# Attention output weights and two gate rows: prepared before the attention stage, or inside the branch stage

## The chip, the cores and the metric

The kernel runs on one core of a Trainium2 chip. A core has five engines that run their own instruction queues side by side: TensorE (PE, matrix products), VectorE (DVE, elementwise work and scans), ScalarE (ACT, copies, casts and activations), GpSimd (POOL) and SyncE (SP, which here only issues transfers). ACT can issue transfers too; an instruction of its queue that has to wait holds up everything behind it. The transfers of all queues run on 16 DMA engines. The metric is the device time of one execution in microseconds (us), as the median of the runs; lower is better.

## What is computed

One step of a one-layer encoder over 1024 prompt frames and 32 sampled frames, 1056 columns in all (`T`), model width 1024:

```
h = rmsnorm(x, g_mix);  q, k, v, cb, cc, cx, ga, gc = split(h @ w_in)
y_attn = stick_breaking(q, k, v) @ w_attn_out        # 512 -> 1024
y_conv = (cb * causal_conv(cc * cx)) @ w_conv_out    # 512 -> 1024
merged = sigmoid(ga) * y_attn + sigmoid(gc) * y_conv
x = x + merged @ w_o
x = x + square(relu(rmsnorm(x, g_ffn) @ w_up)) @ w_down
x = x + sigmoid(rmsnorm(x, g_ple) @ w_ple_gate) * (p @ w_ple)
```

Activations lie transposed, channels on the 128 partitions. A "row" below is a block of 128 channels by 1056 columns (528 KB). The gate `ga` has rows 0 to 7, and so has `gc`; row n of `gd` in DRAM holds row n of `ga`, row n + 8 that of `gc`.

## The kernel before

**Number format.** Every float32 product is made of three matmuls: an operand is split into a high half (a cast by ACT) and a low half (a subtraction by DVE, operand minus high half). So a weight tile costs one ACT and one DVE instruction before PE can use it, and the third matmul of a group is the first that needs the low half.

**Stages.** (1) The input projection runs over pairs of output rows, `SETS` (products named `ps_...i17` for the last pair, gate rows 6 and 7). `seven` does a pair with seven half-size products, and small tasks in the list `side` run one piece after each product. (2) Attention, about 403 to 617 us of the span: 64 steps over 4 head pairs, 2 heads each and 8 query blocks (n is the step's number). Step n makes the scores `z` (PE, line 861), ACT turns them into `r` by a sigmoid (L865), POOL masks them, DVE runs a scan (L879), PE transposes (`pa`, L915), ACT and DVE split the result into `at` (L918, L919), and PE gathers (`av`, L936). There is one buffer for `z` in PSUM, so the next `z` waits until ACT has read the last one. Between the steps PE works off a plan of other products (`fill`), at the start the gate products `ps_g` of rows 0 to 3. (3) The branch stage, about 617 to 687 us, goes through `SEQ_B`: four rows of the convolution output (`c`) and the eight of the attention output (`a`), each of 36 matmuls of 352 columns. For a row, `branch_fetch` loads the weight and the gate row, `branch_high` and `branch_low` split the weight (L984 on ACT, L992 on DVE), `branch_scale` and `branch_sigmoid` finish the gate (L1002 on DVE, L1007 on ACT), `branch_post` multiplies the product by the gate (L1018), `merge_add` adds both branches (L1021), and `merge_high`, `merge_low` and `merge_sums` make the operands of the next stage (L1027, L1031, L1051 to L1059). Six PSUM buffers lie between PE and `branch_post`. (4) The output projection (`ps_woA`, `ps_woS`), from 687 us, whose weights are split at L1561 and L1565. The MLP and the last gate follow, to the end of the span.

**What sets the order.** The order on PE, ACT, DVE and POOL is the order in which the code issues (the blocks under `manual_schedule`). Transfers on SP's queue are placed by a scheduler. All transfers go round eight semaphores; a transfer issued by ACT waits in ACT's queue until the earlier transfer on its semaphore has landed.

**The early tasks.** While the last pair of the input projection runs, `ahead_gate(4)` and `ahead_gate(5)` load gate rows 4 and 5 from `gd`, scale them by the norm factor (DVE), take the sigmoid (ACT) and store them to `gs_`. `ahead_attn(4..7)` load attention output weights 4 to 7, split them and store both halves to `aod`. Both stores are issued by ACT (L649, L638). In the branch stage these rows then need no scale, no sigmoid and no split: the halves come from `aod` as one load (`raw_oa`, L973), and `READY` lists the gate rows that are finished before that stage. The last two gate rows, 6 and 7, stay in SBUF (`last_m`, tiles `m1_i17` and `m2_i17`); they are scaled at attention steps 3 and 4, and at steps 5 and 6 ACT takes the sigmoid and stores them (L1362, L1363).

Of the kernel before, what the change touches and what calls it, by code (L numbers as in the profile page):

```python
# [9 lines left out]
F32 = mybir.dt.float32  # L10
F32R = mybir.dt.float32r
AF = mybir.ActivationFunctionType
# [3 lines left out]
P = 128  # L16
D = 1024
KD = D // P
SEQ = 1024
DEC = 32  # L20
T = SEQ + DEC
# [18 lines left out]
AT2 = (0, 4, 5, 8, 10, 14)  # L40
NEARLY = 4
AT_IN = (4, 8, 10, 12, 14, 18)
READY = (4, 5, 6, 7, 8, 9, 10, 11, 14, 15)
CFILL = 4
ORDER = "LSAFBFG"
START = 2.5
SQ_AT = 96
AHEAD = 6
MM = {mybir.EngineType.Activation, mybir.EngineType.PE, mybir.EngineType.DVE, mybir.EngineType.Pool}


# [1 line left out]
def tile_step(  # L53
# [8 lines left out]
    nc = tc.nc  # L62
# [3 lines left out]
    wraw = ctx.enter_context(tc.tile_pool(name="wraw", bufs=RB))  # L66
    wsp = ctx.enter_context(tc.tile_pool(name="wsp", bufs=2))
    dpool = ctx.enter_context(tc.tile_pool(name="dpool", bufs=1, space=bass.MemoryType.DRAM))

    def blk(name, dt=F32, shape=None):  # L70
        return bpool.tile(shape or [P, T], dt, tag="B", name=name)
# [28 lines left out]
    def raw_w(w, n, kb, name):  # L100
        raw = wraw.tile([P, kb, P], F32, tag="raw", name=f"raw_{name}")
        nc.sync.dma_start(raw, w[n])
        return raw
# [36 lines left out]
    add, sub = ALU.add, ALU.subtract  # L140
    dve, pool = nc.vector.tensor_tensor, nc.gpsimd.tensor_tensor
    raws, ws, side = {}, {}, []
# [174 lines left out]
    def after(n, *gens):  # L317
        for _ in range(n):
            yield
        for g in gens:  # L320
            yield from g
# [15 lines left out]
    SETS = [("g", 12), ("g", 4)] + [(nm, 0) for nm in ("cc", "cx", "cb", "q", "k", "v")] + [("g", 8)]  # L337
# [140 lines left out]
    def md(k, s_):  # L478
        return md_[k, s_ // NP_][s_ % NP_]

    gs_ = dpool.tile([2, P, T], F32, name="gs_")
    aod = dpool.tile([KD, P, 2, 4 * P], F32, name="aod")
    xd = dpool.tile([KD, P, T], F32, name="xd")
    xe = dpool.tile([KD, P, T], F32, name="xe")
    td = [dpool.tile([KD // 2, P, T // 2], F32, name=f"td{k}") for k in range(4)]
# [40 lines left out]
    def scaled(m, by=None):  # L526
        if by is None:
            dve(m, m, rs, op=ALU.mult)
        else:
            nc.vector.scalar_tensor_tensor(m, m, by, rs, op0=ALU.mult, op1=ALU.mult)  # L530
# [89 lines left out]
    def gate_done(n, m):  # L620
        scaled(m)
        yield
        yield
        nc.scalar.activation(m, m, AF.Sigmoid)
        nc.sync.dma_start(gd[n], m)
        yield

    def ahead_attn(n):
        t = blk(f"ao{n}", F32R, [P, 2, 4, P])
        raw = t[:, 1].bitcast(F32)  # L630
        nc.sync.dma_start(raw, w_attn_out[n])
        for _ in range(5):
            yield
        nc.scalar.copy(t[:, 0], raw)
        dve(t[:, 1], raw, t[:, 0].bitcast(F32), op=sub)
        yield
        yield
        nc.scalar.dma_start(aod[n], t.bitcast(F32).rearrange("p e k n -> p e (k n)"))  # L638
        yield

    def ahead_gate(n):
        m = blk(f"ga{n}")
        nc.sync.dma_start(m, gd[n])
        for _ in range(5):
            yield
        scaled(m)
        yield
        nc.scalar.activation(m, m, AF.Sigmoid)
        nc.scalar.dma_start(gs_[n - 4], m)  # L649
        yield  # L650

    def follow(nm, n, ms, wait=0):
# [313 lines left out]

    def branch_fetch(b):
        nm, n = b
        if nm == "c" or n < 4:
            w = raw_w(w_conv_out if nm == "c" else w_attn_out, n, 4, f"o{nm}{n}")  # L970
        else:
            w = wraw.tile([P, 2, 4, P], F32R, tag="raw", name=f"raw_o{nm}{n}")
            nc.sync.dma_start(w.bitcast(F32).rearrange("p e k n -> p e (k n)"), aod[n])  # L973
        sg = blk(f"s{nm}{n}")
        nc.sync.dma_start(sg, gd[n + 8] if nm == "c" else gs_[n - 4] if n in (4, 5) else gd[n])
        fetched[b] = w, sg

    def branch_high(b):
        nm, n = b
        if nm == "a" and n > 3:  # L980
            made[b] = tuple(fetched[b][0][:, i] for i in range(2))
            return
        hi = wsp.tile([P, 4, P], F32R, tag="whi", name=f"whi_o{nm}{n}")
        nc.scalar.copy(hi, fetched[b][0])  # L984
        made[b] = hi

    def branch_low(b):
        nm, n = b
        if nm == "a" and n > 3:
            return  # L990
        lo = wsp.tile([P, 4, P], F32R, tag="wlo", name=f"wlo_o{nm}{n}")
        dve(lo, fetched[b][0], made[b].bitcast(F32), op=sub)  # L992
        made[b] = made[b], lo
# [231 lines left out]
    with tc.manual_schedule(engines=MM):  # L1225
        nc.scalar.preload_act_table_set("sqrt_and_others")
        run(first_gates())
        for s_ in range(2, len(SETS)):
            nm, n = SETS[s_]
            if s_ == 2:  # L1230
                side.append(after(1, stats_x()))
            elif s_ == 4:
                nc.scalar.preload_act_table_set("sigmoid_and_others")
            elif s_ == len(SETS) - 1:
                side.extend(after(AHEAD + i // 2, ahead_gate(n)) for i, n in enumerate((4, 5)))
                side.extend(after(AHEAD + 1 + i // 2, ahead_attn(n)) for i, n in enumerate(range(4, 8)))
            if s_ + 1 < len(SETS):
                side.append(prepare(f"i{s_ + 1}", AT_IN))
            else:
                side.extend([after(4, second_parts(0)), after(6, second_parts(1)), after(4, call(hooks_to, -20)), after(10, call(hooks_to, 0))])  # L1240
            if s_ + 2 < len(SETS):
                side.append(after(5, call(fetch_in, s_ + 2)))
            m = blk(f"m1_i{s_}"), blk(f"m2_i{s_}")
            run(seven(f"i{s_}", *m, copy_of))
            if s_ + 1 < len(SETS):
                follow(nm, n, m, 6 * (s_ == 2))
            else:
                last_m = n, m
        keys_values(0, 0)
        pools[:] = [gps]  # L1250
        run(ahead(START))
        while side:
            run(range(1))
# [99 lines left out]
    with tc.manual_schedule(engines=MM):  # L1353
        queries(0, 0, 0)
        queries(0, 0, 1)
        for n in range(LAST + 3):
            done_f, parts = 0, None
            if n in (3, 4):
                scaled(last_m[1][n - 3])
            elif n in (5, 6):  # L1360
                m = last_m[1][n - 5]
                nc.scalar.activation(m, m, AF.Sigmoid)  # L1362
                nc.scalar.dma_start(gd[last_m[0] + n - 5], m)  # L1363
            if n == 1:
                sample_loads()
            elif n == 3:
                sample_keys()
            if n < LAST:
                i = steps[n][2]
                if i % 2 == 0 and n + 4 < LAST:  # L1370
                    p_, j_, i_ = steps[n + 4]
                    queries(p_, j_, i_ // 2)
                if i == 2 and n + 8 < LAST:
                    keys_values(*steps[n + 8][:2])
            for op in ORDER:
                if op == "S" and n < LAST:
                    scores(*steps[n])
                    if n == LAST - 1:
                        zf = zps.tile([P, 2, 512], F32, tag="z", name="zf")
                        spare_ps.extend(zf[:, h, :] for h in range(2))  # L1380
                elif op == "L":
                    if 1 <= n <= LAST:
                        weigh(*steps[n - 1])
                    for f in pending + split_low:
                        f()
                    pending.clear()
                    split_low.clear()
                elif op == "F" and n < LAST + 2:
                    done_f += 1
                    fill(share[n] + (share[n + 1] - share[n]) * done_f / nf)  # L1390
                    if done_f == 1 and n in SAMPLE_AT:
                        next(sample, None)
                elif op == "G" and n >= 3 and steps[n - 3][2] % 2 == 1:
                    p, j, i_ = steps[n - 3]
                    gather(p, j, i_ // 2)
                elif op in "AB" and 2 <= n <= LAST + 1:
                    if op == "A":
                        parts = flip(*steps[n - 2])
                    next(parts, None)
# [1008 lines left out]
```

## Time and profile before

| | |
|---|---|
| device time, median of 3 runs | 1540.46 us (1539.76 to 1541.39) |
| the profiled execution | 1543.13 us, span from first to last instruction 1541.4 us |
| PE busy | 1511.6 us, 98% of the span |
| DVE, ACT, POOL busy | 1131.5, 763.0, 280.9 us |
| mean granted TensorE clock | 0.995 |
| transfers | 286.83 MB, mean 186 GB/s |

All times below are us from the start of the span. A row of the timeline gives start, duration, engine, line, operation, the tile written and the tiles read (buffer numbers left out), shape and count; in brackets stands how long the engine was idle before the row and who released it. "SPq" and "ACTq" rows are transfers being issued. A row of the windows gives for each engine the busy time and the instructions in that stretch, then the granted TensorE clock, the share of the 16 DMA engines in use and GB/s.

### The profile page before, as it was taken

What the parts mean: (1) busy time and instruction counts of PE and PEld (TensorE: products, weight loads), DVE (VectorE), ACT (ScalarE), POOL (GpSimd) and SP (SyncE); (2) the same over time, 40 slices, a digit from 0 to 9 for tenths busy, and PEclk for the clock granted to TensorE, in tenths of its full rate; (3) what the DMA queues carried; (4) which work ended last, traced back from release to release, by engine and by line L of the source; (5) the groups of instructions that cost most, each with busy time, mean ns of one, the idle gap of its engine ahead of it and who ended that gap; (6) DMA issues with size and microseconds to landing.
All of it is one profiled execution on the core that took longest, in us unless ns stands there. A gap on an engine that the chain in (4) does not pass through costs nothing.

```text
span 1541.4 us, 29904 instructions
## 1 busy us (share of the span) xinstructions
PE 1511.6 (98%) x11888; PEld 1498.2 (97%) x11888; DVE 1131.5 (73%) x1597; ACT 763.0 (50%) x1415; POOL 280.9 (18%) x318
## 2 busy tenths in 40 slices
PE   8999999999899999999999999999999999999997
PEld 8999999999789999999999999999999999999997
DVE  7568666657578988799876677675576986799756
ACT  6544444434456666333375556645543334434654
POOL 2123322231012212000002113222020220000253
PEclk9999999999999999999999999999999999999999
DMA  6513445413946752446755455544886897673443
GB/s 223 202 51 114 190 153 193 166 45 132 311 133 191 253 164 92 168 162 224 267 182 173 159 171 209 193 154 154 300 282 200 277 332 240 205 274 121 140 127 118
DMA packets 121036, 286.83 MB, mean 186 GB/s; under 512 B 13856, under 2 KB 34592, under 8 KB 120896
## 3 DMA queue, kind: packets, MB, share of 16 engines
q1 hardware_dynamic: 119456, 280.34, 54.3%
q10 hardware_dynamic: 1440, 4.58, 0.7%
q8 instruction: 93, 1.52, 0.4%
q14 instruction: 47, 0.39, 0.1%
HBM read 200.98 MB, written 83.89 MB: 185 GB/s over the span
## 4 chain that ended last, share of the span: by engine, by line
PE 59%; DVE 2%; ACT 1%; issue 1%; DMA 0%; SPq 0%; DVEq 0%; ACTq 0%
PE ps_dn L1993 7%; PE ps_dn L1991 7%; PE ps_dn L1992 7%; PE ps_woA L1709 4%; PE ps_A11u L244 2%; PE ps_A11u L242 2%; PE ps_A11u L243 2%; PE ps_pg L120 2%; PE ps_pg L121 2%; PE ps_pg L122 2%; PE ps_S1u L243 2%; PE ps_S1u L244 2%; PE ps_S1u L242 2%; PE ps_woS L1709 2%; PE ps_oa L120 1%; PE ps_oa L122 1%
## 5 line engine op out<-in xcount | busy, mean ns | idle before, releaser
L1993 PE MATMUL ps_dn<-fh,wlo_dn 128*128 128x264 f32 x896 | 255.4, 285 | 0.0
L1992 PE MATMUL ps_dn<-fl,whi_dn 128*128 128x264 f32 x896 | 254.9, 284 | 0.0
L1991 PE MATMUL ps_dn<-fh,whi_dn 128*128 128x264 f32 x896 | 254.8, 284 | 0.0
L1991 PEld LDWEIGHTS ps_dn<-fh,whi_dn 128*128 128x128 f32 x896 | 168.9, 188 | 0.0
L1993 PEld LDWEIGHTS ps_dn<-fh,wlo_dn 128*128 128x128 f32 x896 | 168.8, 188 | 0.0
L1992 PEld LDWEIGHTS ps_dn<-fl,whi_dn 128*128 128x128 f32 x896 | 168.6, 188 | 0.0
L209 POOL TENSOR_TENSOR s_u<-raw_u,raw_u 128x512 f32<-128x512 f32 x22 | 32.1, 1461 | 359.6 <-DVE slS_u L170 284.6
L879 DVE TENSOR_TENSOR_SCAN r<-r 128x128 f32<-128x128 f32 (+3 forms) x64 | 86.5, 1351 | 2.8 <-POOL r L872 2.8
L209 POOL TENSOR_TENSOR s_i<-raw_i,raw_i 128x512 f32<-128x512 f32 x32 | 44.2, 1380 | 239.4 <-DVE slS_i L170 210.3
L1878 ACT CAST whi_dn<-raw_dn 128x1024 fp32r<-128x1024 f32 x40 | 42.0, 1051 | 84.9 <-PE ps_dn L1992 80.9
L1884 DVE TENSOR_TENSOR wlo_dn<-raw_dn,whi_dn 128x1024 fp32r<-128x1024 f32 x40 | 60.9, 1523 | 29.0 <-ACT whi_dn L1878 28.9
L919 DVE TENSOR_TENSOR at<-pa,at 128x512 fp32r<-128x512 f32 (+2 forms) x96 | 52.0, 550 | 31.5 <-ACT at L918 26.9
L242 PE MATMUL ps_A11i<-T,shS_i 128*128 128x264 f32 x256 | 73.1, 286 | 0.0
L244 PE MATMUL ps_A11i<-T,slS_i 128*128 128x264 f32 x256 | 73.0, 285 | 0.0
L243 PE MATMUL ps_A11i<-T,shS_i 128*128 128x264 f32 x256 | 72.8, 284 | 0.0
L170 DVE TENSOR_TENSOR slS_i<-s_i,shS_i 128x512 fp32r<-128x512 f32 x48 | 34.8, 731 | 50.0 <-ACT shS_i L168 49.9
L1904 DVE TENSOR_TENSOR fl<-mr,fh 128x1056 fp32r<-128x1056 f32 x56 | 69.9, 1247 | 0.0
L1753 ACT ACTIVATE m<-m 128x528 f32<-128x528 f32 (+1 forms) x52 | 31.8, 611 | 74.6 <-DVE m L289 30.4
L872 POOL TENSOR_SCALAR_AFFINE_SELECT r<-r 128x128 f32<-128x128 f32 x64 | 30.4, 475 | 201.6 <-ACT r L865 191.4
L2075 POOL TENSOR_TENSOR xx<-xx,pgs 128x384 f32<-128x384 f32 (+1 forms) x23 | 24.2, 1056 | 216.5 <-DVE pgs L2074 209.9
L170 DVE TENSOR_TENSOR slS_u<-s_u,shS_u 128x512 fp32r<-128x512 f32 x48 | 34.3, 715 | 39.8 <-ACT shS_u L168 39.8
L1899 ACT CAST fh<-mr 128x1056 fp32r<-128x1056 f32 x56 | 60.1, 1073 | 0.3 <-DMA mr<-mdB 0.3
(568 smaller groups left out, 5699.0 us busy)
## 6 DMA issues: line engine op xcount, KB each, us to landing
raw_dn<-in_w_down_dram SPq DMA_DIRECT2D x56, 512.0 KB, 4.7
raw_i<-in_w_in_dram SPq DMA_DIRECT2D x36, 512.0 KB, 4.5
mr<-mdT SPq DMA_DIRECT2D x32, 528.0 KB, 5.5
raw_u<-in_w_up_dram SPq DMA_DIRECT2D x32, 512.0 KB, 3.7
mr<-mdB SPq DMA_DIRECT2D x24, 528.0 KB, 6.0
mdB<-m SPq DMA_DIRECT2D x44, 264.0 KB, 2.7
raw_pg<-in_w_ple_gate_dram SPq DMA_DIRECT2D x17, 512.0 KB, 3.6
mdT<-ta SPq DMA_DIRECT2D x32, 264.0 KB, 2.1
```

The costliest lines, as they stand in the source:

```text
L170: dve(l, src, h.bitcast(F32), op=sub)
L209: f()
L242: nc.tensor.matmul(p_, wh[:, k, :], o[:, 0, c], start=new and n == 0, stop=False, **on)
L243: nc.tensor.matmul(p_, wh[:, k, :], o[:, 1, c], start=False, stop=False, **on)
L244: nc.tensor.matmul(p_, wl[:, k, :], o[:, 0, c], start=False, stop=z, **on)
L879: nc.vector.tensor_tensor_scan(rev, rev, rev, 1.0, ALU.mult, ALU.bypass)
L1709: nc.tensor.matmul(on, w[:, i, :], o, start=new and i == n == 0, stop=i == 3 and n == 2, skip_group_check=True,)
L1884: dve(lo, raw, hi.bitcast(F32), op=sub)
L1904: dve(l, mraw.pop(v), opd[v].bitcast(F32), op=sub)
L1991: nc.tensor.matmul(ps, hi[:, j, :], oh, start=j == 0, stop=False)
L1992: nc.tensor.matmul(ps, hi[:, j, :], ol, start=False, stop=False)
L1993: nc.tensor.matmul(ps, lo[:, j, :], oh, start=False, stop=j == NP_ - 1)
```

## The change

The early tasks are taken out. Attention output weights 4 to 7 are loaded raw and split in the branch stage like weights 0 to 3, and gate rows 4 and 5 are scaled and put through the sigmoid there (they leave `READY`). Gate rows 6 and 7 are scaled at attention steps 12 and 20 (`KEEP_AT`), and put through the sigmoid and stored two steps later.

```diff
-READY = (4, 5, 6, 7, 8, 9, 10, 11, 14, 15)
+READY = (6, 7, 8, 9, 10, 11, 14, 15)
-AHEAD = 6
+KEEP_AT = (12, 20)
...
-    def ahead_attn(n):
-        t = blk(f"ao{n}", F32R, [P, 2, 4, P])
-        raw = t[:, 1].bitcast(F32)
-        nc.sync.dma_start(raw, w_attn_out[n])
...
-        nc.scalar.copy(t[:, 0], raw)
-        dve(t[:, 1], raw, t[:, 0].bitcast(F32), op=sub)
...
-        nc.scalar.dma_start(aod[n], t.bitcast(F32).rearrange("p e k n -> p e (k n)"))
-    def ahead_gate(n):
-        m = blk(f"ga{n}")
-        nc.sync.dma_start(m, gd[n])
...
-        scaled(m)
-        nc.scalar.activation(m, m, AF.Sigmoid)
-        nc.scalar.dma_start(gs_[n - 4], m)
...
     def branch_fetch(b):
         nm, n = b
-        if nm == "c" or n < 4:
-            w = raw_w(w_conv_out if nm == "c" else w_attn_out, n, 4, f"o{nm}{n}")
-        else:
-            w = wraw.tile([P, 2, 4, P], F32R, tag="raw", name=f"raw_o{nm}{n}")
-            nc.sync.dma_start(w.bitcast(F32).rearrange("p e k n -> p e (k n)"), aod[n])
+        w = raw_w(w_conv_out if nm == "c" else w_attn_out, n, 4, f"o{nm}{n}")
...
     def branch_high(b):
         nm, n = b
-        if nm == "a" and n > 3:
-            made[b] = tuple(fetched[b][0][:, i] for i in range(2))
-            return
...
     def branch_low(b):
         nm, n = b
-        if nm == "a" and n > 3:
-            return
...
-            if n in (3, 4):
-                scaled(last_m[1][n - 3])
-            elif n in (5, 6):
-                m = last_m[1][n - 5]
-                nc.scalar.activation(m, m, AF.Sigmoid)
-                nc.scalar.dma_start(gd[last_m[0] + n - 5], m)
+            for i_, at_ in enumerate(KEEP_AT):
+                m = last_m[1][i_]
+                if n == at_:
+                    scaled(m)
+                elif n == at_ + 2:
+                    nc.scalar.activation(m, m, AF.Sigmoid)
+                    nc.scalar.dma_start(gd[last_m[0] + i_], m)
```

**ACT at the start of attention.** The rows name line, operation, the tile written and the tile read. `ao` are the early weight tiles, `sg0` and `whi_g1` belong to the gate products of the plan, and `r000` is the first score block of attention. Before:

```order
L721 COPY m2_i17_4614<-ps_A11i17_1_4640 128x264
L634 CAST ao6_4774<-ao6_4774 128x512
L634 CAST ao7_4776<-ao7_4776 128x512
L733 COPY sg0_4884<-ps_g0_0_4885 128x264
L638 DMA aod_159<-ao4_4757 128x1024
L638 DMA aod_159<-ao5_4759 128x1024
L111 CAST whi_g1_4913<-raw_g1_4813 128x1024
L733 COPY sg0_4884<-ps_g0_1_4917 128x264
L638 DMA aod_159<-ao6_4774 128x1024
L638 DMA aod_159<-ao7_4776 128x1024
L865 ACTIVATE r000_4991<-z000_4988 128x128
L865 ACTIVATE r001_5014<-z001_5011 128x256
```

Now, on the same engine at the same place:

```order
L690 ACTIVATE B12_3_4822<-xb1_4734,vecT_98 128x528
L695 COPY m2_i17_4612<-ps_A11i17_0_4619 128x264
L695 COPY m2_i17_4612<-ps_A11i17_1_4638 128x264
L707 COPY sg0_4856<-ps_g0_0_4857 128x264
L111 CAST whi_g1_4883<-raw_g1_4799 128x1024
L707 COPY sg0_4856<-ps_g0_1_4887 128x264
L839 ACTIVATE r000_4959<-z000_4956 128x128
L839 ACTIVATE r001_4982<-z001_4979 128x256
```

Six tasks and six transfers that stood between the last input projection copy and `r000` are gone from ACT's queue.

**ACT at attention steps 4 to 6.** `m1_i17` and `m2_i17` are the kept gate rows, `avl000` is of the first gather, and `r005`, `r006` are score blocks. Before:

```order
L945 COPY avl000_5154<-av000_5148 64x256
L1362 ACTIVATE m1_i17_4613<-m1_i17_4613 128x1056
L1363 DMA gd_143<-m1_i17_4613 128x1056
L865 ACTIVATE r005_5165<-z005_5160 128x768
L918 CAST at00200_5106<-pa0030_5170 128x4x128
L1362 ACTIVATE m2_i17_4614<-m2_i17_4614 128x1056
L1363 DMA gd_143<-m2_i17_4614 128x1056
```

Now, on ACT at steps 12 to 14 of attention, where the first kept row has gone (the second stands eight steps later, ahead of `r106`):

```order
L707 COPY sg1_5106<-ps_g1_3_5442 128x264
L1325 ACTIVATE m1_i17_4611<-m1_i17_4611 128x1056
L1326 DMA gd_143<-m1_i17_4611 128x1056
L839 ACTIVATE r016_5546<-z016_5541 128x896
L892 CAST at01400_5551<-pa0140_5555 128x4x128
```

At the old place `r005` now follows `avl000` directly.

**DVE in the branch stage, from the last convolution row on.** `mg5` is that row times its gate, `sa3` to `sa5` are gate rows of the attention output, `wlo_oa4` is a weight's low half, `s1oS40` a weight of the output projection, and `oB211` an operand of it. Before:

```order
L1018 TENSOR_TENSOR mg5_8343<-ps_oc5_2_8389,sc5_8217 128x352
L1565 TENSOR_TENSOR s1oS40_8423<-sS4o0_8252,s0oS40_8421 128x512
L1018 TENSOR_TENSOR sa3_8285<-ps_oa3_0_8407,sa3_8285 128x352
L1018 TENSOR_TENSOR sa3_8285<-ps_oa3_1_8425,sa3_8285 128x352
L1018 TENSOR_TENSOR sa3_8285<-ps_oa3_2_8439,sa3_8285 128x352
L1021 TENSOR_TENSOR sc3_7138<-sc3_7138,sa3_8285 128x1056
L1031 TENSOR_TENSOR oB211_8472<-sc3_7138,oB211_8472 128x528
```

Now:

```order
L983 TENSOR_TENSOR mg5_8311<-ps_oc5_2_8357,sc5_8185 128x352
L967 TENSOR_TENSOR sa4_8307<-sa4_8307,rs_140 128x1056
L957 TENSOR_TENSOR wlo_oa4_8392<-raw_oa4_8305,whi_oa4_8375 128x512
L1528 TENSOR_TENSOR s1oS40_8397<-sS4o0_8220,s0oS40_8395 128x512
L983 TENSOR_TENSOR sa3_8253<-ps_oa3_0_8377,sa3_8253 128x352
L983 TENSOR_TENSOR sa3_8253<-ps_oa3_1_8399,sa3_8253 128x352
L983 TENSOR_TENSOR sa3_8253<-ps_oa3_2_8413,sa3_8253 128x352
L986 TENSOR_TENSOR sc3_7106<-sc3_7106,sa3_8253 128x1056
L967 TENSOR_TENSOR sa5_8373<-sa5_8373,rs_140 128x1056
L957 TENSOR_TENSOR wlo_oa5_8453<-raw_oa5_8371,whi_oa5_8431 128x512
L996 TENSOR_TENSOR oB211_8448<-sc3_7106,oB211_8448 128x528
```

Two scales and two low halves stand in between; the low halves of weights 6 and 7 follow in the same way after the merges of rows 4 and 5. On ACT, the sigmoid of `sa4` now stands right ahead of the cast that `s1oS40` needs (`s0oS40`).

More of the change, by code (lines that the diff above doesn't have):

```diff
@@ L479, in md @@
         return md_[k, s_ // NP_][s_ % NP_]
-    gs_ = dpool.tile([2, P, T], F32, name="gs_")
-    aod = dpool.tile([KD, P, 2, 4 * P], F32, name="aod")
     xd = dpool.tile([KD, P, T], F32, name="xd")
@@ L625, in gate_done @@
         nc.sync.dma_start(gd[n], m)
-        yield
-    def ahead_attn(n):
-        t = blk(f"ao{n}", F32R, [P, 2, 4, P])
-        raw = t[:, 1].bitcast(F32)
-        nc.sync.dma_start(raw, w_attn_out[n])
-        for _ in range(5):
-            yield
-        nc.scalar.copy(t[:, 0], raw)
-        dve(t[:, 1], raw, t[:, 0].bitcast(F32), op=sub)
[L636 to L639, printed above, removed]
-    def ahead_gate(n):
-        m = blk(f"ga{n}")
-        nc.sync.dma_start(m, gd[n])
-        for _ in range(5):
-            yield
-        scaled(m)
-        yield
-        nc.scalar.activation(m, m, AF.Sigmoid)
-        nc.scalar.dma_start(gs_[n - 4], m)
         yield
@@ L968, in branch_fetch @@
         nm, n = b
-        if nm == "c" or n < 4:
-            w = raw_w(w_conv_out if nm == "c" else w_attn_out, n, 4, f"o{nm}{n}")
-        else:
-            w = wraw.tile([P, 2, 4, P], F32R, tag="raw", name=f"raw_o{nm}{n}")
-            nc.sync.dma_start(w.bitcast(F32).rearrange("p e k n -> p e (k n)"), aod[n])
+        w = raw_w(w_conv_out if nm == "c" else w_attn_out, n, 4, f"o{nm}{n}")
         sg = blk(f"s{nm}{n}")
-        nc.sync.dma_start(sg, gd[n + 8] if nm == "c" else gs_[n - 4] if n in (4, 5) else gd[n])
+        nc.sync.dma_start(sg, gd[n + 8] if nm == "c" else gd[n])
         fetched[b] = w, sg
@@ L1233, in tile_step @@
                 nc.scalar.preload_act_table_set("sigmoid_and_others")
-            elif s_ == len(SETS) - 1:
-                side.extend(after(AHEAD + i // 2, ahead_gate(n)) for i, n in enumerate((4, 5)))
-                side.extend(after(AHEAD + 1 + i // 2, ahead_attn(n)) for i, n in enumerate(range(4, 8)))
             if s_ + 1 < len(SETS):
```

## The prediction

> **What bounds the kernel now.** I read the page first, then the waits by engine, then the windows of 2 us around the waits found, and last the timelines of PE, ACT and DVE there. The first two:
>
> ```profile
> PE 1511.6 (98%) x11888; PEld 1498.2 (97%) x11888; DVE 1131.5 (73%) x1597; ACT 763.0 (50%) x1415; POOL 280.9 (18%) x318
> PE z L861 <- ACT r L865: 7.0, 2, 4.3
> ```
>
> PE is the bound over the whole span, so a change is worth what it takes from PE's idle time or from its slow clock, and costs what it adds to them. The largest wait inside the kernel is that of the attention scores `z` for ACT. Here are PE's waits where attention begins, and one of a later step:
>
> ```profile
> 395.72 0.39 PE L729 MATMUL ps_g<-B,whi_g 128*128 128x264 f32 x1 [1.23 <-ACT m_i L721]
> 403.04 0.30 PE L861 MATMUL z<-ks,q 128*128 128x128 f32 x1 [1.07 <-ACT ao L634]
> 410.12 0.58 PE L861 MATMUL z<-ks,q 128*128 128x256 f32 x1 [4.35 <-ACT r L865]
> 426.25 0.74 PE L861 MATMUL z<-ks,q 128*128 128x448 f32 x1 [2.66 <-ACT r L865]
> ...
> 443.95 1.10 PE L936 MATMUL av<-at,vv 128*128 128x256 f32 x7 [0.65 <-DVE at L919]
> ```
>
> Four waits within 31 us, 9.31 us together. What follows two of them is seen in the windows (the granted clock is the number ahead of the last two):
>
> ```profile
> 408.00:410.00 2.00, 0.00 (x0) 0.00 (x0) 0.51 (x1) 0.21 (x1) 0.00 (x0) 0.71 0.70 187
> ...
> 414.00:416.00 2.00, 2.00 (x10) 1.94 (x9) 1.08 (x2) 1.12 (x6) 0.58 (x3) 0.58 1.04 396
> ...
> 424.00:426.00 2.00, 0.00 (x0) 0.00 (x0) 0.00 (x0) 0.61 (x1) 0.00 (x0) 0.98 0.91 313
> ...
> 428.00:430.00 2.00, 2.00 (x14) 2.00 (x13) 1.43 (x2) 1.43 (x3) 0.58 (x3) 0.67 0.96 353
> ```
>
> A mean of 0.71 over 2 us is half clock for 1.16 us, so the first slow stretch goes from 408.84 to 415.68 (0.58 is half for 1.68 us). The second goes from 425.92 (0.98) to 429.32 (0.67). PE works at half clock from 410.12 to 415.68 and from 426.25 to 429.32, and loses half of that: 2.78 and 1.54 us. With the waits, 13.63 us are lost here.
>
> **Early tasks and the kept rows leave the start of attention.** What PE waited for is in ACT's timeline:
>
> ```profile
> 393.10 0.74 ACT L716 ACTIVATE B<-xb,vecT 128x528 fp32r<-128x528 f32 x1 [7.67 <-PE ps_A11i L244]
> ...
> 403.21 2.96 ACTq L638 DMA_DIRECT2D aod<-ao  x2
> 406.21 1.04 ACT L111 CAST whi_g<-raw_g 128x1024 fp32r<-128x1024 f32 x1 [2.93 <-DMA aod<-ao]
> 407.16 0.37 ACT L733 COPY sg<-ps_g 128x264 f32<-128x264 f32 x1
> 407.38 2.37 ACTq L638 DMA_DIRECT2D aod<-ao  x2
> 409.79 0.28 ACT L865 ACTIVATE r<-z 128x128 f32<-128x128 f32 x1 [2.26 <-DMA aod<-ao]
> ...
> 424.96 0.33 ACTq L1363 DMA_DIRECT2D gd<-m_i  x1
> 425.39 0.81 ACT L865 ACTIVATE r<-z 128x768 f32<-128x768 f32 x1 [3.01 <-DMA q<-qd]
> ```
>
> The score of step 0 was made at 403.04, but ACT read it only at 409.79, because four stores of `aod` stood ahead in its queue and two of them waited for older transfers (2.93 and 2.26 us). That is the wait of 4.35. The wait of 1.07 is a copy behind the casts of `ao`. The wait of 2.66 is `r005` behind the store of the first kept row (3.01). The wait of 1.23 is a copy behind the cast of row 393.10, whose input `xb` was issued on SP behind two early loads (`ga`) and landed among four more (`ao`); in the new order it waits for its load alone. All four causes leave these places: 12 transfers, six casts and sigmoids on ACT, six DVE instructions, and two of each for the kept rows. SP loses six issues, so `xb`, `ks` and `q` go out earlier. All of 13.63 us is open to be won.
>
> What is late next? The chain from `r` over POOL, the scan and `at` to the gather, which costs 0.65 at 443.95, with the DVE as full as it will be here. I leave one such wait in place of the four: gain 12.98. The ends are 0 (all four waits come back for another reason) and 13.63.
>
> [...]
>
> **Kept rows at steps 12 to 14 and 20 to 22.** Each costs DVE one scale, and ACT a sigmoid and an issue. The rows next to the new places:
>
> ```profile
> 454.91 0.92 ACT L865 ACTIVATE r<-z 128x896 f32<-128x896 f32 x1 [0.49 <-PE z L862]
> 479.76 0.92 ACT L865 ACTIVATE r<-z 128x896 f32<-128x896 f32 x1 [1.42 <-PE z L862]
> 386.00:430.00 44.00, 34.68 (x247) 32.64 (x246) 23.09 (x31) 19.64 (x40) 3.04 (x13) 0.88 0.98 311
> 440.00:482.00 42.00, 41.35 (x345) 39.60 (x344) 32.55 (x49) 23.28 (x54) 6.99 (x30) 1.00 0.44 132
> ```
>
> These are `r016` and `r106`, ahead of which the sigmoids now stand. ACT was idle there, and it is busy for 23.28 of 42 us. The DMA engines are used to 0.44 rather than 0.98, so the store should find its older transfer landed. I take 0. The cover is ACT's idle time; if it fails, `r016` is late and the next `z` with it. Ends: 0, and one wait like the one at 426.25 with its clock, 4.20, for each row.
>
> **The branch stage.** DVE gets two scales and four low halves more, ACT four casts and two sigmoids. ACT has room; DVE has little:
>
> ```profile
> 656.27 1.25 DVE L1002 TENSOR_TENSOR sa<-sa,rs 128x1056 f32<-128x1056 f32 x1
> 657.44 0.68 DVE L992 TENSOR_TENSOR wlo_oa<-raw_oa,whi_oa 128x512 fp32r<-128x512 f32 x1
> ...
> 659.40 0.69 DVE L1565 TENSOR_TENSOR s1oS<-raw_wp,s0oS 128x512 fp32r<-128x512 f32 x1
> 660.01 0.69 DVE L1565 TENSOR_TENSOR s1oS<-sS2o,s0oS 128x512 fp32r<-128x512 f32 x1
> 660.61 1.38 DVE L1018 TENSOR_TENSOR mg<-ps_oc,sc 128x352 f32<-128x352 f32 x3
> 661.91 0.68 DVE L1565 TENSOR_TENSOR s1oS<-sS4o,s0oS 128x512 fp32r<-128x512 f32 x1
> ...
> 664.35 0.53 DVE L1018 TENSOR_TENSOR sa<-ps_oa,sa 128x352 f32<-128x352 f32 x1 [0.90 <-PE ps_oa L122]
> ...
> 666.92 1.33 DVE L1031 TENSOR_TENSOR oB<-sc,oB 128x528 fp32r<-128x528 f32 x2 [0.75 <-ACT oB L1027]
> ...
> 674.29 0.71 DVE L1031 TENSOR_TENSOR oB<-mg,oB 128x528 fp32r<-128x528 f32 x1 [0.76 <-ACT oB L1027]
> ...
> 679.09 1.33 DVE L1031 TENSOR_TENSOR oB<-mg,oB 128x528 fp32r<-128x528 f32 x2 [0.76 <-ACT oB L1027]
> ...
> 695.75 0.68 DVE L1565 TENSOR_TENSOR w1oA<-raw_A12o,w0oA 128x512 fp32r<-128x512 f32 x1
> ```
>
> From start to start a scale takes 1.17 us (656.27 to 657.44) and a low half 0.61 (659.40 to 660.01). That is 2 x 1.17 + 4 x 0.61 = 4.78 us more on DVE. ACT adds to it:
>
> ```profile
> 657.56 1.09 ACT L1007 ACTIVATE sa<-sa 128x1056 f32<-128x1056 f32 x1 [0.53 <-DVE sa L1002]
> 658.55 0.60 ACT L1561 CAST s0oS<-raw_wp 128x512 fp32r<-128x512 f32 x1
> ```
>
> The scale of row 4 takes the place at 661.91 and ends at 663.16; ACT then does its sigmoid (0.99 to the next row) and only then the cast for `s1oS` (0.62), which ends at 664.81. DVE would reach that subtraction at 661.91 + 1.17 + 0.61 = 663.69 and stands for 1.16 us (0.04 for the hand-over). The DVE's idle times between here and 690 take up 0.90 + 0.75 + 0.76 + 0.76 = 3.17. What is left is a lag of 4.78 + 1.16 - 3.17 = 2.77 us. Does PE feel it?
>
> ```profile
> 676.08 0.32 PE L122 MATMUL ps_oa<-o0h,raw_oa 128*128 128x352 f32 x1
> ...
> 696.49 0.39 PE L1709 MATMUL ps_woA<-oB,w1oA 128*128 128x264 f32 x1
> ```
>
> The weight's low half of row 695.75 is ready at 696.43, and PE takes it at 696.49: 0.06 us of slack, and DVE has no idle time ahead of it in which to catch up. So PE loses 2.77 - 0.06 = 2.7 us by then. About 1 us of it shows earlier, at 676.08, the third matmul of output row 6, whose low half now stands behind the merge of row 4; none of these waits reaches the 2.66 us after which the clock fell above, so no slow stretch is added. Ends: 1.5 us without ACT's part (4.78 - 3.17 - 0.06), and 5.9 with no idle time used (4.78 + 1.16). The four loads of 512 KB become 256 KB; nothing waits for them in these rows, and I take 0. Row 4's low half is done at 663.77, ahead of PE.
>
> **Sum.** 12.98 won, 2.7 lost: 10.3 us. The profiled execution took 1543.13 us, 2.67 above the median of the runs shown, and would take 1532.8; from the median of 1540.46 it comes to 1530.2.
>
> **Rivals.**
> 1. *A load becomes the wait.* The sampled frames' keys (`kk`, the view of that tile) took long from issue to landing, and landed just as PE reached them:
>
> ```profile
> DMA to landing us min/median/max: 8.4/8.9/9.1
> ```
>
> PE now comes some 10 us earlier. For it: they still stand behind nine `q` loads on SP. Against: in the stretch 386 to 430 the DMA engines carry 6.4 MB less (six gate row transfers of 528 KB, four of 256 and four of 512 KB) of 13.7 (44 us at 311 GB/s). One wait like that at 426.25, 4.20 with its clock: 1534.4.
> 2. *ACT waits again at step 14 or 22.* For: the same instruction pair waited for 3.01 us. Against: 0.44 of the DMA engines. 4.20 each: 1534.4 or 1538.6.
> 3. *The branch stage hides its part* (six PSUM buffers let PE run ahead). Against: the slack of 0.06. 1540.46 - 12.98 = 1527.5.
> 4. *Slower: the loads, not ACT's queue, set the start of attention.* Then PE waits there as before, nothing is won, and the branch stage's 2.7 to 5.9 come on top: 1543.2 to 1546.4. It decides once the start gives less than 2.7. For: 0.98 of the DMA engines in 386 to 430. Against: step 0's score was ready for ACT for over 6 us.
>
> **How the numbers follow.** The forecast as described 0.66 (1526.8 to 1534.5, from 13.63 won at no loss to 12.98 won with 5.9 lost and a little more), rival 1 0.10, rival 2 0.08, rival 3 0.05, rival 4 0.11. A measurement tells about 0.2% from no change, 3.1 us: faster is below 1537.4, slower above 1543.5. Rival 4 straddles the second bound: 0.06 same, 0.05 slower. The rest is faster, 0.89. The range of 1526.5 to 1537 leaves out rival 4 and the double wait of rival 2.
>
> **What would show it.** In the changed kernel PE should reach the second score (now 410.12) near 403.5 with no half clock before it; ACT should have no wait for `aod`, and none over 0.5 us at steps 14 and 22; DVE should run without a break from row 4's scale to the output projection, with PE waits of about 1 us at row 6's weight and 1 to 2 us at `w1oA`. It is wrong if `z` or the sample scores wait for a transfer, or if the branch stage loses more than 6 us.

## The result and the profile after

The changed kernel takes 1532.49 us (median of 4 runs, 1531.79 to 1533.14) beside 1540.93 for the kernel before (4 runs, 1539.76 to 1543.95). The ratio is 0.9942, 95% interval 0.9925 to 0.9959: faster by 0.4 to 0.8%. Beside other runs of the kernel before, the changed kernel came to 1531.77 and a ratio of 0.9932 (0.9918 to 0.9946; e10 below). The forecast was 1530.2, a ratio of 0.9933. The profiled execution took 1533.14 us, with a span of 1531.4.

The page's line of busy times:

```profile
PE 1507.8 (98%) x11888; PEld 1494.7 (98%) x11888; DVE 1131.2 (74%) x1597; ACT 764.1 (50%) x1415; POOL 279.9 (18%) x318
```

PE is busy for 3.8 us less with as many matmuls: at half clock they are busy for longer (in the kernel before a 128x264 product of `ps_g` takes 0.42 us at 410.94, where the clock is 0.50, and 0.28 at 416.53, where it is 1.00). All waits of PE over 0.14 us from 394 to 480 and from 600 to 700, from its timeline in the changed kernel:

```profile
429.74 1.10 PE L910 MATMUL av<-at,vv 128*128 128x256 f32 x7 [0.65 <-DVE at L893]
...
605.25 0.43 PE L120 MATMUL ps_oc<-cv,whi_oc 128*128 128x352 f32 x1 [0.57 <-DVE oT L1371]
662.76 0.43 PE L122 MATMUL ps_oa<-o0h,wlo_oa 128*128 128x352 f32 x1 [0.93 <-DVE wlo_oa L957]
674.77 0.39 PE L1672 MATMUL ps_woA<-oB,wlo_wo 128*128 128x264 f32 x1 [0.23 <-DVE wlo_wo L1482]
679.53 0.39 PE L1672 MATMUL ps_woA<-oB,whi_wo 128*128 128x264 f32 x1 [0.36 <-DVE oB L996]
684.96 0.39 PE L1672 MATMUL ps_woA<-oB,w1oA 128*128 128x264 f32 x1 [0.32 <-DVE w1oA L1528]
```

The four waits at the head of attention are gone. The gather's wait of 0.65 stands where it stood before (443.95 then). Four waits in the branch stage and the projection are new. Three rows of the kernel before mark the same places:

```profile
372.27 0.39 PE L242 MATMUL ps_A11i<-T,shA_i 128*128 128x264 f32 x1 [0.38 <-DVE m_i L296]
...
619.53 0.43 PE L120 MATMUL ps_oc<-cv,whi_oc 128*128 128x352 f32 x1 [0.58 <-DVE oT L1408]
...
1532.67 0.88 PE L2131 MATMUL prl<-dgl,ones 96*128 96x96 f32 x6 [0.40 <-DVE dgl L2130]
```

And two of the changed kernel:

```profile
372.55 0.39 PE L242 MATMUL ps_A11i<-T,shA_i 128*128 128x264 f32 x1 [0.39 <-DVE m_i L296]
...
1521.66 1.52 PE L2094 MATMUL prl<-dgl,ones 96*128 96x96 f32 x6 [0.39 <-DVE dgl L2093]
```

Read as differences of start: the changed kernel is 0.28 us late at 372, 14.21 us early at the gather, 14.28 at the first branch product, 11.53 at `w1oA` (696.49 before) and 11.01 at the last product. So the head of attention gave 14.5 us, attention itself nothing more, the branch stage took 2.75 back, and the rest 0.5. From the start of the last product the changed kernel's span had 9.7 us left and the other's 8.7, so the spans differ by 10.0. At that end the granted clock falls to half in both, in the changed kernel while the last product runs (0.85 from 1521 to 1522, then 0.50; the product takes 1.52 us) and in the other only behind it (0.63 from 1535 to 1536, then 0.50; the product takes 0.88). The code is the same there.

The windows of both kernels from 386 to 432 show the other part of the gain, the clock (the number after POOL's column). Before:

```profile
386.00:432.00 46.00, 36.68 (x260) 34.42 (x259) 24.87 (x33) 20.57 (x43) 3.04 (x13) 0.89 0.94 300
```

Changed:

```profile
386.00:432.00 46.00, 45.35 (x371) 43.58 (x370) 31.29 (x48) 22.84 (x53) 5.31 (x23) 1.00 0.69 203
```

PE issues 371 matmul records instead of 260 in the same 46 us, the clock is 1.00 instead of 0.89, and the DMA engines are used to 0.69 instead of 0.94. DVE in the branch stage, from the changed kernel's timeline:

```profile
647.61 1.25 DVE L967 TENSOR_TENSOR sa<-sa,rs 128x1056 f32<-128x1056 f32 x1
648.77 0.69 DVE L957 TENSOR_TENSOR wlo_oa<-raw_oa,whi_oa 128x512 fp32r<-128x512 f32 x1
650.52 0.69 DVE L1528 TENSOR_TENSOR s1oS<-sS4o,s0oS 128x512 fp32r<-128x512 f32 x1 [1.06 <-ACT s0oS L1524]
```

DVE stands 1.06 us for the cast that ACT makes behind the sigmoid of row 4; from there to 690 its timeline marks no other idle time.

### The profile page after: what moved, and what is told of

It is laid out like the page before. It is cut to its first block, busy times and chain, and to the rows that moved or that the text cites. A ratio compares the mean times of both kernels' runs of the same rounds, so it can differ in the third digit from the quotient of the medians.

```text
span 1531.4 us, 29875 instructions
## 1 busy us (share of the span) xinstructions
PE 1507.8 (98%) x11888; PEld 1494.7 (98%) x11888; DVE 1131.2 (74%) x1597; ACT 764.1 (50%) x1415; POOL 279.9 (18%) x318
## 3 DMA queue, kind: packets, MB, share of 16 engines
q8 instruction: 93, 1.52, 0.4%
## 4 chain that ended last, share of the span: by engine, by line
PE 58%; DVE 4%; ACT 1%; issue 1%; DMA 0%; DVEq 0%; SPq 0%; ACTq 0%
PE ps_dn L1956 7%; PE ps_dn L1955 7%; PE ps_dn L1954 7%; PE ps_woA L1672 3%; PE ps_A11u L244 3%; PE ps_A11u L243 3%; PE ps_A11u L242 3%; PE ps_pg L120 2%; PE ps_pg L121 2%; PE ps_pg L122 2%; PE ps_S1u L243 2%; PE ps_S1u L242 2%; PE ps_S1u L244 2%; PE ps_woS L1672 2%; PE ps_S2u L243 1%
```

## Experiments

Each was timed beside the kernel before (four or five runs, e1 twelve). The last four columns are worked out from the starts of the same PE matmuls in the trace of the kernel before and in the trace of the run: what each stretch gained (+) or lost (-), by the times before, in us. In the last of them the code is the same in all kernels; it shows how far single executions differ.

| kernel | median us | ratio to before, 95% | 365 to 443 (head) | 443 to 619 | 619 to 700 (branch) | 700 to end |
|---|---|---|---|---|---|---|
| changed | 1532.49 | 0.9942 (0.9925 to 0.9959) | +14.5 | +0.1 | -2.8 | -0.5 |
| e1 kept rows moved alone | 1540.81 | 0.9993 (0.9985 to 1.0001) | +3.2 | +0.1 | +0.2 | -0.8 |
| e2 early tasks out alone | 1533.20 | 0.9947 (0.9934 to 0.9960) | +13.6 | +0.1 | -2.8 | -0.7 |
| e3 early work without stores | 1533.68 | 0.9952 (0.9940 to 0.9963) | +12.6 | 0.0 | -2.7 | -0.5 |
| e4 gates early | 1530.10 | 0.9926 (0.9914 to 0.9938) | +13.6 | -0.1 | +0.4 | -0.3 |
| e5 scales on POOL | 1533.22 | 0.9938 (0.9924 to 0.9951) | +14.7 | +0.1 | -3.8 | -1.6 |
| e6 cast ahead of sigmoid | 1531.01 | 0.9920 (0.9908 to 0.9933) | +14.5 | +0.1 | -1.6 | -0.4 |
| e7 gates at steps 32, 40 | 1529.06 | 0.9909 (0.9896 to 0.9923) | +14.8 | -1.3 | +0.2 | +0.3 |
| e8 weights early | 1533.08 | 0.9937 (0.9925 to 0.9950) | +12.4 | 0.0 | -2.2 | +0.3 |
| e9 gates at steps 26, 53 | 1532.53 | 0.9938 (0.9925 to 0.9950) | +14.7 | -5.2 | +0.3 | -0.1 |
| e10 changed again | 1531.77 | 0.9932 (0.9918 to 0.9946) | +14.7 | 0.0 | -2.8 | -0.5 |
| e11 gates at steps 36, 40 | 1527.54 | 0.9899 (0.9882 to 0.9915) | +14.8 | 0.0 | +0.2 | +0.6 |
| e12 gates at steps 40, 44 | 1527.68 | 0.9900 (0.9886 to 0.9915) | +14.8 | -0.6 | +0.2 | +1.4 |

**e1 and e2: one half of the change at a time.** e1 is the kernel before with the new `KEEP_AT` code; e2 is the changed kernel with the old code for the kept rows.

```diff
 # e1, against the kernel before
+KEEP_AT = (12, 20)
-            if n in (3, 4):
-                scaled(last_m[1][n - 3])
...
+            for i_, at_ in enumerate(KEEP_AT):
...
 # e2, against the changed kernel: the same lines the other way round
```

> The kernel before, with only the two kept gate rows moved to steps 12 to 14 and 20 to 22; the early tasks stay. Theory (each wait at the head has its own cause, and the store of the kept row made the wait of 2.66 us and the half clock behind it): 2.66 + 1.54 = 4.2 us are gained, 1540.9 - 4.2 = 1536.7, the second score still waits 4.35 us for ACT and the first slow stretch stays. Rival (the transfers of the early tasks crowd the DMA engines until about 430 us, and another transfer is late in its place): PE still waits 2 to 3 us near 420 and the time is 1540 to 1541.

> The changed kernel with the kept rows put back to steps 3 to 6; the early tasks are out. Theory of parts that add up: the store of the kept row waits on ACT as before, the sixth score is late by 2.7 us and the clock falls, 1532.5 + 4.2 = 1536.7. Rival (interaction: that store waited only because the early transfers held its semaphore's older transfer up): ACT's wait for it stays under 0.5 us and the time is that of the changed kernel, 1532 to 1533.

Both came out at their rivals' times: e1 gained 0.07% (0.9985 to 1.0001, not told from nothing), and e2 is the changed kernel within the error. PE's waits in e1, from its timeline:

```profile
394.75 0.39 PE L730 MATMUL ps_g<-B,whi_g 128*128 128x264 f32 x1 [0.92 <-ACT m_i L722]
402.06 0.30 PE L862 MATMUL z<-ks,q 128*128 128x128 f32 x1 [1.06 <-ACT ao L635]
410.19 0.58 PE L862 MATMUL z<-ks,q 128*128 128x256 f32 x1 [5.37 <-ACT r L866]
424.04 0.44 PE L862 MATMUL z<-ks,q 128*128 128x448 f32 x1 [1.15 <-DMA q<-qd]
```

The store of the kept row is gone, but a score still waits near 424, now for the load of its `q`, and PE's wait behind the stores of `aod` is longer (5.37 for 4.35; ACT waits 3.02 and 3.21 there for 2.93 and 2.26). The wait near 424 is 1.15 and not the 2 to 3 of the rival, and no half clock follows it (1.00 from 416 to 432): in the head this one execution gains 3.2 us on the traced one of the kernel before. The medians of 12 and 17 runs do not show so much; 0.15%, 2.3 us, is the most that their interval leaves. In e2 the kept rows' stores stand where they stood, and ACT does not wait (its timeline):

```profile
412.12 0.36 ACTq L1325 DMA_DIRECT2D gd<-m_i  x1
412.58 0.81 ACT L839 ACTIVATE r<-z 128x768 f32<-128x768 f32 x1 [0.49 <-ACT m_i L1324]
```

0.49 us for what took 3.01 before. So the kept row was the place where the wait showed, and the early tasks were its cause. That it was their transfers is argued, from the load that PE waits for in e1.

**e3: the early work without its stores.** Loads, casts, low halves, scales and sigmoids stand where they stood; nothing is stored, and the branch stage does not use them.

```diff
+    def ahead_attn(n):     # as before, without nc.scalar.dma_start(aod[n], ...)
+    def ahead_gate(n):     # as before, without nc.scalar.dma_start(gs_[n - 4], m)
```

> The changed kernel with the early loads, casts, scales, low halves and sigmoids put back where they were, but without their stores; the results are not used, and the branch stage does its own work as in the changed kernel. Theory (the stores in ACT's queue made the large wait): the waits of 1.23 and 1.07 us come back, the second score does not wait and no half clock follows, 1532.5 + 2.3 = 1534.8. Rival (the volume of early loads or the casts set the start of attention): the second score waits over 3 us and the half clock comes back, 1532.5 + 2.3 + 4.35 + 2.78 = 1541.9.

PE's waits at the head of attention in e3:

```profile
394.75 0.39 PE L724 MATMUL ps_g<-B,whi_g 128*128 128x264 f32 x1 [0.56 <-ACT m_i L716]
401.97 0.30 PE L856 MATMUL z<-ks,q 128*128 128x128 f32 x1 [0.97 <-DMA q<-qd]
```

The second score does not wait, as the theory had it; the two waits ahead of it came back smaller, 0.56 and 0.97 for 1.23 and 1.07. The early loads, casts and sigmoids cost 1.9 us of the head (14.5 - 12.6), and the stores most of the rest. No run issued the same stores from another queue; what points at ACT's queue rather than at the stores' bytes is the order on ACT in the kernel before, where `r` stands right behind a store that waits 2.26 us.

**e4 and e8: gates alone, weights alone.** e4 brings only `ahead_gate` back into the changed kernel (with `gs_` and rows 4, 5 in `READY`), e8 only `ahead_attn` (with `aod`).

```diff
 # e4
+READY = (4, 5, 6, 7, 8, 9, 10, 11, 14, 15)
+                side.extend(after(AHEAD + i // 2, ahead_gate(n)) for i, n in enumerate((4, 5)))
 # e8
+                side.extend(after(AHEAD + 1 + i // 2, ahead_attn(n)) for i, n in enumerate(range(4, 8)))
```

> The changed kernel with only the gate rows 4 and 5 prepared early again, with their stores to DRAM by ACT; the weights stay in the branch stage. Theory (the branch stage loses 2.6 us since DVE has 4.78 us more work and stands 1.06 us for ACT, and 3.17 us of idle time take up the rest): without the two scales and the sigmoid DVE has 2.44 us more and stands for nothing, so the branch stage loses 0 to 0.3, while the wait of 1.23 at the first gate product may come back: 1532.5 - 2.5 + 1.2 = 1531.2, without that wait 1530.0. Rival (two stores in ACT's queue are enough to hold attention up): the second score waits over 2 us again and the time is 1533 to 1536.

> The changed kernel with only the weights 4 to 7 prepared early again, with ACT's stores of both halves; gates 4 and 5 stay in the branch stage, the kept rows at their new steps. Theory (these four stores of 512 KB, waiting in ACT's queue, are what holds the second score): it waits 3 to 5 us again and half clock follows, 4.35 + 2.78 = 7.1 lost, 2.4 of the branch stage's 2.6 won: 1537.2. Rival (gates and weights together crowd the DMA engines, either alone does not): the stores wait under 1 us and the time is 1530 to 1531.

e4 went as its theory had it: a wait of 0.76 came back at the first gate product, the branch stage has no wait over 0.14 us, and by the trace it is 2.3 us ahead of the changed kernel (0.9 lost in the head, 3.2 won in the branch stage); the medians go the same way, though the intervals of the ratios overlap. e8 fits neither theory. ACT's timeline in e8:

```profile
400.00 3.10 ACTq L638 DMA_DIRECT2D aod<-ao  x2
403.15 0.28 ACT L854 ACTIVATE r<-z 128x128 f32<-128x128 f32 x1 [2.82 <-DMA aod<-ao]
```

PE's:

```profile
403.48 0.39 PE L850 MATMUL z<-ks,q 128*128 128x256 f32 x1 [1.16 <-ACT r L854]
...
409.67 1.64 PE L1261 MATMUL zs<-kk,qs 64*32 64x288 f32 x16
```

And DVE's in the branch stage:

```profile
652.11 0.69 DVE L1554 TENSOR_TENSOR s1oS<-sS4o,s0oS 128x512 fp32r<-128x512 f32 x1 [1.66 <-ACT s0oS L1550]
...
663.85 0.71 DVE L1020 TENSOR_TENSOR oB<-mg,oB 128x528 fp32r<-128x528 f32 x1 [0.76 <-ACT oB L1016]
```

The stores hold ACT for 2.82 us, much as before, but they stand in its queue 7 us earlier (the last pair at 400.00, not 407.38), because no sigmoid of a gate row waits ahead of them; so PE loses 1.16 and no clock (1.00 from 400 to 416). Most of the other 0.9 us of the head goes at the 16 sampled scores `zs`, which take 1.64 us here and 0.72 in the changed kernel: the loads of their keys `kk` into PE wait 0.63 for the transfer, which landed 5.7 us after its issue (3.7 there). That is rival 1 of the prediction on a small scale. The branch stage lost 2.2 and not the 0.2 expected: without low halves DVE comes to the cast of `s0oS` earlier and stands 1.66 for it, and two of its waits of 0.76 for `oB` stay. In each of these DVE waits for ACT to cast what its own merge has just made, so only work between the merge and the subtraction fills the wait; work ahead of the merge moves both.

**e6: ACT's order in the branch stage.**

```diff
-                branch_sigmoid(nxt)
+                if nxt != ("a", 4):
+                    branch_sigmoid(nxt)
...
             for f in BESIDE.get(i, ()):
                 f()
+            if nxt == ("a", 4):
+                branch_sigmoid(nxt)
```

> The changed kernel with ACT's sigmoid of gate row 4 moved behind the cast of the output projection's weight (s0oS), for which DVE stood 1.06 us. Theory (DVE runs without a break from there on, so what it stood is lost in full): 1532.5 - 1.06 = 1531.4, and PE's wait at row 6's weight, 0.93, is gone. Rival (the stand only took time that DVE would have waited for PE or ACT a little later): 1532.5.

The branch stage's loss fell from 2.8 to 1.6 and the wait at row 6's weight is gone, as the theory had it; by the medians the step (0.9920 beside 0.9942 and 0.9932) is small beside the intervals, which overlap, so it is the trace that shows it.

**e5: the two scales on POOL.**

```diff
         if gate_ready(b):
             return
-        dve(sg, sg, rs, op=ALU.mult)
+        if b not in (("a", 4), ("a", 5)):
+            dve(sg, sg, rs, op=ALU.mult)
 # and in branch_fetch, right behind the load
+        if b in (("a", 4), ("a", 5)):
+            pool(sg, sg, rs, op=ALU.mult)
```

> The changed kernel with the scales of gate rows 4 and 5 in the branch stage done by POOL, right after their loads, instead of by DVE; POOL does nothing else there. Theory (the branch stage's loss is DVE work): DVE loses 2 x 1.17 = 2.34 us of work, so the loss of 2.6 goes down to 0.3 to 1.3 and the time is 1530 to 1531. Rival (what counts is the sigmoid ahead of the cast on ACT, or POOL slows DVE down): PE's waits at row 6's weight and the output projection stay and the time is 1532 to 1533.

The loss grew to 3.8. POOL's timeline in e5:

```profile
636.56 2.58 POOL L947 TENSOR_TENSOR sa<-sa,rs 128x1056 f32<-128x1056 f32 x1 [38.92 <-DMA sa<-gd]
```

DVE's:

```profile
636.76 2.94 DVE L959 TENSOR_TENSOR wlo_oc<-raw_oc,whi_oc 128x512 fp32r<-128x512 f32 x1
```

And PE's:

```profile
639.75 0.43 PE L122 MATMUL ps_oc<-cv,wlo_oc 128*128 128x352 f32 x1 [1.75 <-DVE wlo_oc L959]
```

A DVE subtraction that takes 0.69 us in the changed kernel took 2.94: it started while POOL ran and ended 0.56 after POOL did (639.14). Its low half was what PE needed next. Two windows of e5 show that this wait of 1.75 us took the clock as well:

```profile
640.00:642.00 2.00, 2.00 (x10) 2.00 (x10) 1.97 (x5) 0.00 (x0) 0.00 (x0) 0.61 0.40 131
642.00:644.00 2.00, 2.00 (x9) 2.00 (x9) 1.97 (x3) 0.35 (x1) 0.00 (x0) 0.53 0.55 135
```

By 0.61 and 0.53, PE ran at half clock from 640.44 to 643.88 (its products of 352 columns start 0.29 to 0.30 apart there and 0.16 apart behind it). Half of these 3.44 us, 1.72, is an estimate from the clock of what that cost. With the wait of 1.75 and one of 0.33 at `w1oA` that is the 3.8. PE's waits at row 6's weight and at the first two places of the projection are gone, but PE came there 3.5 us later, so e5 does not show what the scales alone cost. It shows the rival's second half in this place: beside POOL the subtraction took 2.94 us for 0.69.

**e7, e9, e11, e12: gates 4 and 5 prepared within attention.** The early gate task moves behind the crowded stretch (`gs_` and `READY` as in e4); only the steps differ.

```diff
+GATE_AT = (32, 40)    # e7; e9 (26, 53), e11 (36, 40), e12 (40, 44)
+                if n == at_ - 4:
+                    early[i_] = blk(f"ga{i_}")
+                    nc.sync.dma_start(early[i_], gd[4 + i_])
+                elif n == at_:
+                    scaled(early[i_])
+                elif n == at_ + 2:
+                    nc.scalar.activation(early[i_], early[i_], AF.Sigmoid)
+                    nc.scalar.dma_start(gs_[i_], early[i_])
```

> The changed kernel with gate rows 4 and 5 prepared in the middle of attention: loaded at steps 28 and 36, scaled at 32 and 40, put through the sigmoid and stored by ACT two steps later, so that the branch stage only loads them. Theory (the branch stage's loss goes as it did with early gates, and ACT and DVE have room in attention away from the crowded transfers): no wait at the first gate product, none in the branch stage, 1532.5 - 2.6 = 1529.9. Rival (DVE is over 80% busy in attention, and two scales of 1.17 us there make PE wait for the next scan or gather): 1 to 2.3 us come back, 1531 to 1532.

> Gate rows 4 and 5 prepared in attention as in the kernel before this one (e7), but scaled at steps 26 and 53 instead of 32 and 40, where DVE was idle for 1.85 of 6 us (476 to 482) and 1.59 of 6 us (560 to 566) in the changed kernel. Theory (at step 32 DVE was busy for 9.94 of 10 us, so the scale of 1.17 us made PE wait for gathers; that is the 1.28 us which e7's attention took longer): that loss goes, and the time is 1.2 us under e7's, 1527.9, a ratio of 0.990 to the kernel before. Rival (two scales cost attention as much anywhere, since the chain of scans is tight): the same as e7.

> Gate rows 4 and 5 prepared in attention, scaled at steps 36 and 40 (e7 had 32 and 40, and its trace lost 1.28 us between 503 and 516 by the times before, around step 32, and 0.1 around step 40; e9 with 26 and 53 lost 1.4 and 3.7). Theory (the cost hangs on whether the engine that gets the work is the one that PE waits for at that step, and step 36's scale falls where DVE was idle for 1.3 of 6 us): under 0.5 us is lost in attention, the branch stage loses nothing, 1528 to 1529, a ratio of 0.990 to 0.991. Rival (every further step costs about 1.3 us in attention): as e7 or slower, 1529 to 1530.

> The same with steps 40 and 44. Theory: step 40 costs nothing as in e7; at step 44 DVE was busy for 5.45 of 6 us (530 to 536), so its scale costs up to 0.6 us: 1528 to 1529. Rival: 1.3 us and more are lost there, or the sigmoid at step 46 holds PE up as the one at step 55 did in e9: 1530 to 1532.

In all four the branch stage lost nothing. e7 lost 1.3 us around step 32, between theory and rival. e9's theory failed: the places with the most idle DVE time were the dearest. The first row lost about 1.6 us around steps 26 to 28, at two waits for DVE's `r` (0.21 and 0.65, the latter 0.18 in the changed kernel) and one of 0.50 for ACT, which takes the row's sigmoid first there. The second row's sigmoid at step 55 lost the rest. ACT's timeline there:

```profile
569.09 1.09 ACT L1337 ACTIVATE ga<-ga 128x1056 f32<-128x1056 f32 x1
...
572.75 0.40 ACT L801 COPY em<-ps_pw 128x264 f32<-128x264 f32 x1
```

PE's timeline in e9:

```profile
573.21 0.43 PE L1056 MATMUL ps_oc<-cv,cw 128*128 128x352 f32 x1 [2.38 <-ACT em L801]
```

And e9's windows (the clock is the number behind POOL's column):

```profile
573.00:574.00 1.00, 0.79 (x5) 0.79 (x5) 1.00 (x3) 0.15 (x1) 0.00 (x0) 0.86 0.07 25
574.00:576.00 2.00, 2.00 (x11) 2.00 (x10) 2.00 (x2) 0.86 (x2) 1.24 (x1) 0.50 0.95 322
...
577.00:578.00 1.00, 1.00 (x9) 1.00 (x8) 0.00 (x0) 0.38 (x1) 0.00 (x0) 0.93 0.00 0
```

PE waited 2.38 us for a copy that stood behind the sigmoid, and half clock followed. In the changed kernel the same product waits 0.47 for that copy. ACT was the engine that PE waited for at that step, and I had looked at DVE's idle time alone. e11 lost nothing (0.0 in attention) and is the fastest kernel here, 1527.54 us, 1.0% under the kernel before (0.9899, 0.9882 to 0.9915). e12 lost 0.6, by its trace one wait for DVE of 1.27 instead of 0.73; by the medians it equals e11.

**e10: the changed kernel once more.**

> The changed kernel once more, beside the same runs of the kernel before as e9, to see how far the gain of one traced execution (10.0 us by the spans) is from that of the medians. If the kernel before varies from run to run by what its transfers do at the head of attention, its runs scatter over 3 us or more and the changed kernel's over less than 2, and the ratio comes to 0.993 to 0.995 again.

As expected: the kernel before scattered over 3.65 us in these runs (1540.62 to 1544.27), the changed kernel over 1.34 (1531.27 to 1532.61), and the gain of the medians was 10.4 us instead of 8.4. The forecast of 10.3 lies in the interval of both measurements (0.9933 in 0.9925 to 0.9959 and in 0.9918 to 0.9946).

## Why the prediction was right, point by point

1. **What holds the head of attention: ACT's queue.** Right for the large wait: e3 keeps the early loads and the work and drops the stores, and the second score no longer waits. In the changed kernel that score starts 0.6 us before the 403.5 of the forecast (PE's timeline):

```profile
402.91 0.28 PE L835 MATMUL z<-ks,q 128*128 128x256 f32 x1
```

Wrong for the wait at 426.25, which the prediction put down to "the store of the first kept row" and wanted to win by moving it: e2 leaves it in place and wins it, e1 moves it and wins 0.07%, with another wait in its place. The cause was the early tasks, by e1 most likely their transfers, which held up whatever came next. The 4.20 us of this wait came in by luck: the change also takes the early tasks out, and by e2 that alone is enough.
2. **Its size.** Forecast 12.98, measured 14.5. The mis-sized term is "one such wait left in their place": none came, and the gather's 0.65 was there before. By the starts of the same matmuls the parts gave 1.6, 1.5, 4.4, 2.7, 2.8 and 1.5 us, for 1.23, 1.07, 4.35, 2.78, 2.66 and 1.54 in the forecast; so the first two waits gave 0.8 more than their idle time. The kernel before's PE timeline shows why: ahead of row 395.72 the matmuls start 0.12 apart and last 0.28, so the marked idle of 1.23 begins at the end of the last one (394.49), 0.16 after the next would have started; and behind it they start 0.22, 0.14 and 0.23 apart before they come back to 0.12. That makes 0.16 + 0.23, some 0.4 us beyond the bracket.
3. **Kept rows: 0.** Right, from ACT's timeline of the changed kernel, at steps 14 and 22:

```profile
441.55 0.92 ACT L839 ACTIVATE r<-z 128x896 f32<-128x896 f32 x1 [0.40 <-ACT m_i L1325]
...
465.55 0.92 ACT L839 ACTIVATE r<-z 128x896 f32<-128x896 f32 x1 [0.50 <-PE z L836]
```

But e9 shows that this price belongs to those steps: the same pair of instructions at step 55 set off 2.38 us and a slow stretch. And by e2 the move was not needed.

4. **Branch stage: 2.7.** Measured 2.75 to 2.8. The part of ACT (forecast 1.16, stood 1.06) is 1.2 by e6, and what is left without it, 1.6, is the forecast's lower end of 1.5. The wait at row 6's weight is 0.93 (forecast about 1). The rest came as 0.23, 0.36 and 0.32 at three products, not as 1 to 2 at `w1oA` alone; the four waits add up to 1.84, and the other 0.9 fits what four waits cost beyond their brackets (point 2). One step was right only by chance: 3.17 us of DVE's idle time were set against any added work, but e8 shows that the waits for `oB` take up only work that stands between the merge and the subtraction. The low halves of weights 6 and 7 stand there, right ahead of the 0.76s; scales ahead of the merge do not. That no slow stretch was added is right, as the longest wait was 0.93; but the 2.66 us that the prediction held these waits against is no safe bound, since 2.38 was enough in e9 and 1.75 in e5.
5. **From one execution to the median.** The trace's difference of 10.0 was a good guide, yet the two medians gave 8.4 and 10.4. The kernel before scatters, and the changed one does so less (3.65 and 1.34 us in e10).
6. **Rivals.** The sampled keys (rival 1) landed in time (the view of that tile, changed kernel):

```profile
DMA to landing us min/median/max: 3.6/3.7/3.8
```

That is 3.7 us for 8.9, from an issue at 401.7 to 403.1 instead of 407.8 to 410.5. Why it is faster was not tested; in e8, with the weights' transfers back, it was 5.7. Rival 2 is refuted by the rows of point 3, rival 3 by the four waits of the branch stage, rival 4 by e3. Rival 4 holds a grain of truth: 1.9 us of the head belong to loads and work rather than to stores (e3).

## What to carry to other kernels

A wait's releaser names the instruction that was last, not the one to move: take the suspect out alone and leave it in alone (e1, e2) before its price goes into a sum. What early preparation cost hung on the place here: the same two gate rows cost 0.9 us at the crowded head (e4, where the DMA engines were used to 0.90 from 400 to 416), nothing at steps 36 and 40 (e11, 0.58 from 432 to 600), and some 3 us in the branch stage (-2.8 beside +0.2). For each place, ask which engine PE waits for at that step, and read a wait as cover only for work that can be put inside it, between the instruction that starts it and the one that ends it.

## What was not expected of the hardware

- **POOL held DVE up.** In e5 a subtraction of two SBUF tiles took 2.94 us instead of 0.69 beside a POOL multiplication of 2.58 us. Beside the second POOL multiplication (651.62 to 654.08) a DVE product that reads one input from PSUM took its usual 0.53 us, and a merge of two SBUF tiles 1.76 instead of 1.26. I had read POOL's idleness as room. What makes DVE wait was not shown.
- **Waits shorter than 2.66 us took the clock.** 2.38 us of idle PE time (e9) halved it, and so did 1.75 us (e5); waits of 1.16 (e8), 1.23 (before) and 1.27 (e12) did not (the clock is 1.00 from 400 to 416 in e8 and from 394 to 398 before; in e12 the products behind the wait start 0.12 apart, as they do at full clock). The windows of e9 put its slow stretch at 573.72 (0.86) to 577.14 (0.93), and those of e5 at 640.44 to 643.88, 3.4 us long like the one of 425.92 to 429.32; the other of the prediction was 6.84, twice that. In e9 and e5 the clock fell only after PE had gone on, 0.5 and 0.7 us behind the end of the wait. What sets these lengths, and which wait is long enough, was not shown.
- **Early transfers went with scatter.** Kernels with early transfers at the head scattered most from run to run: 4.3 us (before, 17 runs), 5.7 (e1, 12 runs), 4.1 (e3), 3.0 (e8) and 2.6 (e4), five runs each; those without by 0.5 (e6) to 2.3 (e9). The runs are few and none was made to separate the cause.
